# A two-layer gating and Mamba-2 trunk: scan chunks in pairs, split products in the order of their parts, and the output projection's scalings a part later

## The chip, the cores and the metric

The kernel runs on one core of one Trainium2 chip. The metric is the device time of one execution in microseconds (us). The engines have short names here: PE is TensorE's matmul, PEld its weight load, DVE is VectorE, ACT is ScalarE, POOL is GpSimd and SP is SyncE, which here only issues DMAs.

## The reference, cut to what matters

Two layers, each `h = h + W_out(mixer(rmsnorm(h)) * silu(z))`, and a final RMSNorm, on 1024 tokens of width 1024, all in float32. Layer A mixes by causal spatial gating in chunks of 128 tokens. Layer B is a Mamba-2 SSD mixer with 8 groups of 4 heads, a state of 128 and chunks of 128 tokens. What the change touches most is its scan, per group and chunk:

```python
cb = einsum('bclgn,bcsgn->bclsg', Cm, Bm)
w_ls = cb[..., None] * decay * dt[:, :, None]
y_diag = einsum('bclsgj,bcsgjp->bclgjp', w_ls, x)
states = einsum('bclgn,bclgj,bclgjp->bcgjpn', Bm, decay_to_end * dt, x)
# over the chunks: carry = carry * chunk_decay + state
y_off = einsum('bclgn,bcgjpn,bclgj->bclgjp', Cm, prev, exp(dA_cs))
y = y_diag + y_off + x * d_skip
gated = rmsnorm_per_group(y * silu(z))
out = gated @ w_out
```

## The kernel before, in words

Every float32 matrix product is made of three cheaper ones: both operands are split into a high part `h` and a low part `l` (`split`: ACT copies the high part, DVE or POOL subtracts it), and `mm3` issues hh, then h with one low part, then the other low part with h, for each piece of the contraction (L134, L135 and L136 of the profile). The large projections are not plain products either. `Block` (the input projections) and `Out` (the output projections `ao` of layer A and `bo` of layer B) use a scheme of seven half-size products (numbered 1 to 7) whose operands are sums of the blocks of the matrices; a product is worked in four parts `c` of 256 contraction rows, and the parts are prepared on ACT and DVE while PE is on an earlier one. `prep` splits a part's operands (L742 for DVE's half), `post` empties a product's accumulators.

The order is written by hand. Each engine executes its own list of instructions in the order in which the program issues them; nothing is moved by a scheduler. Buffers come from tagged pools: `sm` has four PSUM buffers, `k2` has four buffers for the decay tile `wl`, `q4` six, `k1` three for the state and `t1`.

The stages in time: a head (to 62 us), the blocks of layer A (to 530), its output projection `ao` (to 691), the passage to layer B and the first of its blocks (to 1007), the scan (to 1342), and the output projection `bo` with the final norm (to 1511). `scans` runs 64 chunks, eight groups of eight, and in between `project` issues what is left of layer B's input projection, in ticks of six products (`ab`), and then product 1 of `bo`. `want` says how many ticks are due after each half chunk. So PE's list alternates between a chunk's small float32 products and a few ticks.

For chunk `n`, before the change, the loop issues in this order: `pe_b(n)` (on PE the off-diagonal product with the state of the chunk before, L1626, the chunk's own state, L1633, and the diagonal, L1636, whose two heads of a pair go to the two column halves of the array; and in every fourth chunk the sums of squares, L1702), half a chunk of ticks, `pe_a(n+2)` (transposes and C.B, L1593 and L1594), `weights(n+1)` (DVE: `wl` times C.B, L1617), `update(n)` (DVE: the state, L1656), `out(n)` (DVE: L1668 and the skip L1671), `decay(n+2)` (ACT: L1599 and L1601), `carry(n+1)` (POOL, L1647), one `drain` of the convolution's queue (a tap on DVE is L1322), `tokens(n+2)` (DVE: L1607 and L1609) and `gate(n)` (POOL, L1674). Then SP gets `load(n+3)` (L1588: the decay of 128 columns spread over the partitions, 256 KB) and, in chunks 1 and 5 of a group, `prefetch` (`xbc`, 1 MB, L1554, for four of the groups; z, L1557; four spreads of exp(dA), L1561) for the next half group.

`hook_b` holds what `bo` does per product and part: loads (`get`), the scalings of its operands by the group norms (`ready`, L1755 on DVE), and sums of operand blocks (`plus`, `add`, L762).

Of the kernel before, what the change touches and what calls it, by code (L numbers as in the profile page):

```python
# [29 lines left out]
def kernel(  # L30
# [151 lines left out]
    class Block:  # L182
# [83 lines left out]
        def mm(self, n, i, post=True, halves=(0, 1)):  # L266
# [395 lines left out]
    class Out:  # L662
# [11 lines left out]
        def __init__(self, src, w, scale, res, accs, keep, order):  # L674
# [3 lines left out]
            self.Y3, self.negs = [], []  # L678
# [113 lines left out]
        def product(self, n, hook=None):  # L792
# [18 lines left out]
            for c in range(4):  # L811
# [45 lines left out]
        def last_mm(self, i):  # L857

            o = self.acc[3] = self.acc[5]
            Yh, Yl = zip(*self.Y3)  # L860
            if (3, i) not in self.ops:
                self.prep_unit(i)
            X = self.ops.pop((3, i))
            for k in range(8):
                mm3(o[i], [m[:, k, :] for m in X], [m[k // 4][:, k % 4, :] for m in (Yh, Yl)],
                    False, k == 7, True)
# [530 lines left out]
    def projections():  # L1397
# [21 lines left out]
        def push(g, kind, m, a):  # L1419
# [9 lines left out]
            if queue:  # L1429
                queue[-1] += ops.pop(0)  # L1430
# [118 lines left out]
    def prefetch(g, th):  # L1549

        st = sts[g]
        if g in xbc_d:
            t = st["xbc", th] = s8([P, 4, 512], "xbc")
            nc.sync.dma_start(out=t, in_=xbc_d[g][:, th])  # L1554
# [9 lines left out]
    class Scan:  # L1564


        def __init__(self, g, eng):
            self.g, self.st, self.eng = g, sts[g], eng
            self.wl, self.tp, self.cw, self.ps, self.state = {}, {}, {}, {}, {}
# [50 lines left out]
        def pe_b(self, c, ends=None):  # L1620

            w, wl = self.cw[c], self.wl.pop(c)
            yy = sm("yy")
            if c > 0:
                for pt in range(2):
                    nc.tensor.matmul(out=yy[:, 256 + pt * P:384 + pt * P],  # L1626
                                     lhsT=self.state[c - 1][:, pt * P:(pt + 1) * P], rhs=self.x(3, c),
                                     start=True, stop=True)
            sp = None
            if c < 7 or ends is not None:  # L1630
                sp = sm("sp")
            if c < 7:
                nc.tensor.matmul(out=sp[:, 0:256], lhsT=w[:, 512:640], rhs=w[:, 256:512], start=True, stop=True)  # L1633
            for j in range(4):
                pt, f = j // 2, j % 2
                nc.tensor.matmul(out=yy[f * 64:(f + 1) * 64, pt * P:(pt + 1) * P], lhsT=w[:, j * 64:(j + 1) * 64],  # L1636
                                 rhs=wl[:, j, :], start=True, stop=True)
            if ends is not None:
                ends.sum_b(sp[:, 256:512], 2 if ends.g == G - 1 else 1)
            self.ps[c] = yy, sp  # L1640
# [10 lines left out]
        def update(self, c):  # L1651
            if c == 0:
                self.state[0] = k1([P, 256], "state")
                V.tensor_copy(out=self.state[0], in_=self.ps[0][1][:, 0:256])
            elif c < 7:
                V.tensor_tensor(out=self.state[c], in0=self.ps[c][1][:, 0:256], in1=self.state[c], op=ALU.add)  # L1656
# [7 lines left out]
        def out(self, c):  # L1664
            yy, t2 = self.ps.pop(c)[0], self.y(c)
            if c > 0:
                t1 = k1([P, 2, P], "t1")
# [353 lines left out]
```

## Time and profile before

| What | us |
|---|---|
| median of 3 runs (range) | 1514.28 (1512.39 to 1514.48) |
| the profiled execution | 1512.85 |
| its span, first to last instruction | 1511.1 |
| PE busy in the span | 1471.6 (97%) |
| DVE, ACT, POOL busy | 1053.7, 783.3, 401.5 |
| PE's first matmul | 9.7 |

An engine's busy share says how much of the span it spent in instructions. PE's matmuls overlap, so a matmul row's duration (0.39 for 512 columns) is longer than the distance from one start to the next; distances between starts are what PE takes. A row of several records (`x8`) shows the start of the first. A bracket at a row's end gives the idle time ahead of it and the instruction whose end released it.

### The profile page before, as it was taken

The page shows a single profiled execution, that of the slowest core. Times are in us where ns is not written, and L with a number is a line of the kernel's source. Part 1 is how long each engine was busy: PE and PEld are TensorE (multiplying, and loading weights), DVE is VectorE, ACT ScalarE, POOL GpSimd, SP SyncE. Part 2 cuts the span into 40 slices and gives each one's busy share as a digit, 9 for nine tenths or more (in the row PEclk, how much of TensorE's full clock was granted, in tenths as well). Part 3 has the DMA queues.
Part 4 walks back from the last instruction along what each step waited for, and adds up shares of the span by engine and source line. Part 5 has one row for each costly group of instructions (what it writes and reads, how often), then busy time and mean ns, then how long its engine had stood idle before and what let it go on. Part 6 is the DMA issues. An engine that isn't in the chain of part 4 may idle for free. (4 is left out here: it accounts for less than half of the span.)

```text
span 1511.1 us, 21297 instructions
## 1 busy us (share of the span) xinstructions
PE 1471.6 (97%) x7834; PEld 1222.5 (81%) x7834; DVE 1053.7 (70%) x1713; ACT 783.3 (52%) x1256; POOL 401.5 (27%) x451
## 2 busy tenths in 40 slices
PE   6899999999999999999999999999999999999997
PEld 6899988888888888877878888877777777777875
DVE  7966567665666655678666467867677787688876
ACT  6533332222323445565565566666676666756463
POOL 1111110000000023202131222217576766633121
PEclk9999999999999999999999999999999999999999
DMA  5554322322222999957377978677655565579973
GB/s 183 141 168 140 106 97 103 117 103 103 101 79 96 337 262 246 258 145 162 104 174 154 208 154 167 142 242 209 183 160 183 160 187 141 169 255 275 255 156 112
DMA packets 174952, 254.45 MB, mean 168 GB/s; under 512 B 16400, under 2 KB 103168, under 8 KB 171648
## 3 DMA queue, kind: packets, MB, share of 16 engines
q1 hardware_dynamic: 124768, 168.93, 36.0%
q0 software_dynamic: 42448, 70.27, 23.2%
q10 hardware_dynamic: 7632, 13.90, 2.6%
q8 instruction: 62, 1.02, 0.3%
q14 instruction: 42, 0.34, 0.1%
HBM read 186.14 MB, written 51.18 MB: 157 GB/s over the span
## 5 line engine op out<-in xcount | busy, mean ns | idle before, releaser
L134 PE MATMUL acc<-hh,wh 128*128 128x512 f32 x868 | 339.9, 392 | 0.9 <-ACT u L296 0.9
L136 PE MATMUL acc<-hh,wl 128*128 128x512 f32 x868 | 338.4, 390 | 2.0 <-DVE wl L112 1.8
L135 PE MATMUL acc<-hl,wh 128*128 128x512 f32 x868 | 337.9, 389 | 0.0
L112 DVE TENSOR_TENSOR wl<-wr,wh 128x1024 fp32r<-128x1024 f32 (+1 forms) x96 | 114.3, 1193 | 118.3 <-ACT wh L111 118.1
L136 PEld LDWEIGHTS acc<-hh,wl 128*128 128x128 f32 x868 | 162.9, 188 | 37.9 <-DVE wl L112 3.7
L134 PEld LDWEIGHTS acc<-hh,wh 128*128 128x128 f32 x868 | 163.1, 188 | 34.9 <-ACT u L296 1.7
L135 PEld LDWEIGHTS acc<-hl,wh 128*128 128x128 f32 x868 | 163.1, 188 | 33.1
L296 ACT COPY u<-acc 128x512 f32<-128x512 f32 x115 | 66.8, 583 | 197.8 <-PE acc L136 197.7
L111 ACT CAST wh<-wr 128x1024 fp32r<-128x1024 f32 (+1 forms) x112 | 115.2, 1030 | 94.4 <-PE acc L135 56.9
L136 PE MATMUL acc<-wh,hl 128*128 128x256 f32 x448 | 129.2, 288 | 4.1 <-DVE hl L407 3.7
L134 PE MATMUL acc<-wh,hh 128*128 128x256 f32 x448 | 129.6, 289 | 2.9 <-DVE wh L418 1.3
L135 PE MATMUL acc<-wl,hh 128*128 128x256 f32 x448 | 128.5, 287 | 1.3 <-DVE wl L421 1.3
L134 PE MATMUL ab<-hh,wh 128*128 128x512 f32 x288 | 124.7, 433 | 1.2 <-DVE zt L999 0.7
L136 PE MATMUL ab<-hh,wl 128*128 128x512 f32 x288 | 113.2, 393 | 0.0
L135 PE MATMUL ab<-hl,wh 128*128 128x512 f32 x288 | 112.7, 391 | 0.0
L136 PEld LDWEIGHTS acc<-wh,hl 128*128 128x128 f32 x448 | 87.6, 196 | 5.4 <-DVE hl L407 4.4
L134 PEld LDWEIGHTS acc<-wh,hh 128*128 128x128 f32 x448 | 87.8, 196 | 3.8 <-ACT hh L400 1.6
L135 PEld LDWEIGHTS acc<-wl,hh 128*128 128x128 f32 x448 | 87.8, 196 | 1.7 <-DVE wl L421 1.5
L1599 ACT ACTIVATE wl<-wl,tk 128x128 f32<-128x128 f32 x256 | 81.6, 392 | 3.0 <-DMA wl<-cs_d 2.7
L649 POOL DMA_DIRECT2D y_d<-y x8 | 4.4, 549 | 290.8 <-DVE y L646 290.8
L135 PE MATMUL bo<-wl,xh 128*128 128x512 f32 x192 | 75.8, 395 | 3.8 <-DVE wl L742 2.1
L112 DVE TENSOR_TENSOR wl<-t,wh 128x1024 fp32r<-128x1024 f32 (+1 forms) x38 | 45.5, 1196 | 47.5 <-ACT wh L111 47.4
(317 smaller groups left out, 3250.6 us busy)
## 6 DMA issues: line engine op xcount, KB each, us to landing
wr<-in_a_w_in_dram SPq DMA_DIRECT2D x48, 512.0 KB, 3.6
wl<-cs_d SPq DMA_DIRECT2D x64, 256.0 KB, 3.6
wr<-in_b_w_in_dram SPq DMA_DIRECT2D x30, 512.0 KB, 7.4
wb<-in_a_w_out_dram SPq DMA_DIRECT2D x10, 1024.0 KB, 11.7
wb<-in_b_w_out_dram SPq DMA_DIRECT2D x10, 1024.0 KB, 11.1
wr<-in_b_w_in_dram SPq DMA_DIRECT2D x36, 256.0 KB, 5.9
v<-v_d SPq DMA_DIRECT2D x8, 1024.0 KB, 5.1
y_d<-y POOLq DMA_DIRECT2D x8, 1024.0 KB, 5.8
```

Source lines behind the costliest of these rows:

```text
L111: nc.scalar.copy(out=hi, in_=src)
L112: return (eng or nc.vector).tensor_tensor(out=lo, in0=src, in1=hi.bitcast(F32), op=ALU.subtract)
L134: nc.tensor.matmul(out=o, lhsT=l[0], rhs=r[0], start=start, stop=False, **kw)
L135: nc.tensor.matmul(out=o, lhsT=l[0], rhs=r[1], start=False, stop=False, **kw)
L136: nc.tensor.matmul(out=o, lhsT=l[1], rhs=r[0], start=False, stop=stop, **kw)
L296: nc.scalar.copy(out=self.u[n][:, i], in_=a)
L649: store = lambda: nc.gpsimd.dma_start(out=y_d[-1], in_=y)
L1599: nc.scalar.activation(wl[:, j, :], wl[:, j, :], AF.Relu, scale=-1.0, bias=tokc(2, c, self.g)[:, j:j + 1])
```

## The change

Four things are edited.

In `scans`, the chunks are issued in pairs. `pe_b` is taken apart into `own` (the state's product, L1658 after), `off` (L1667) and `diagonal`, which makes the eight products of two chunks in one row (L1650), with both chunks' results in one PSUM buffer. An even chunk issues own, off, the diagonal of itself and the next, the sums of squares where due, and the two loads of `wl` for chunks n+4 and n+5; an odd one own and off. `pe_a`, `decay` and `tokens` are now three chunks ahead, `weights` two, `update` stands ahead of `weights`, and `out` is split into `skip` and `out`. The even iteration drains the convolution's queue twice, as the odd one does. `prefetch` is split into two parts, the `xbc` part in the first chunk of each half group and the z and exp(dA) part in the second, both for the half group that starts four chunks after the first; `push` puts a convolution's first step ahead of, instead of behind, what the queue's last entry holds.

On SP the names are: `wl` the decay load, `wr` the raw weights of a later block, `xbc`, `ze` the z load and the spreads, `g_d` the gated output's store. Before, at the first chunks of the scan:

```order
L120 DMA wr<-in_b_w_in_dram 128x4x256
L1588 DMA wl<-cs_d 128x512 x3
L1554 DMA xbc<-xbc_d_6209 128x2048
L1557 DMA ze<-z_d_5287 128x2x512
L1561 DMA ze<-ecs_d 64x512 x4
L1588 DMA wl<-cs_d 128x512 x2
```

and now, at the same place:

```order
L120 DMA wr<-in_b_w_in_dram 128x4x256
L1610 DMA wl<-cs_d 128x512 x2
L1575 DMA xbc<-xbc_d_6209 128x2048
L1579 DMA ze<-z_d_5287 128x2x512
L1583 DMA ze<-ecs_d 64x512 x4
L1610 DMA wl<-cs_d 128x512 x4
```

Of the three `wl` loads that stood ahead of this `xbc` before, one, for chunk 4, takes a buffer that PE has to free, and it is chunk 0's; now both of the two do, and their buffers are those of the chunks 0 and 1, which the first paired diagonal reads.

On PE, two chunks of a spilled group before, from one chunk's products to the ticks behind them:

```order
L136 MATMUL ab<-hh,wl 128x512
L1626 MATMUL yy<-xbc,state 128x128 x2
L1633 MATMUL sp<-cw 128x256
L1636 MATMUL yy<-wl,cw 64x128 x4
L134 MATMUL ab<-hh,wh 128x512
```

and now, an odd chunk, the ticks and transposes behind it, and the even chunk that follows:

```order
L1658 MATMUL os<-cw 128x256
L1667 MATMUL os<-xbc,state 128x128 x2
L134 MATMUL ab<-hh,wh 128x512
L135 MATMUL ab<-hl,wh 128x512
L136 MATMUL ab<-hh,wl 128x512
L134 MATMUL ab<-hh,wh 128x512
L135 MATMUL ab<-hl,wh 128x512
L136 MATMUL ab<-hh,wl 128x512
L1615 MATMUL tp<-ident,xbc 128x128 x3
L1616 MATMUL tp<-xbc 128x128
```

```order
L136 MATMUL ab<-hh,wl 128x512
L1658 MATMUL os<-cw 128x256
L1667 MATMUL os<-xbc,state 128x128 x2
L1650 MATMUL yy<-wl,cw 64x128 x8
L134 MATMUL ab<-hh,wh 128x512
```

The diagonals' four products per chunk have become eight per pair, at the even chunk alone.

In `Block.mm`, `Out.product` and `Out.last_mm`, the three kinds of split product are no longer issued together for each contraction piece: all hh products of a part come first, then those with the part that is ready next, then the rest. In the last part of a product of `Out` the accumulators are finished one after the other.

In `hook_b`, for product 2, `ready(1, 0, c)` is put into a list `after` that `product` works off behind the preparation of the part, and the sum of the blocks of part `c` is made a part later. On DVE, around product 2's first parts (`ya` the gated operand that is scaled or summed, `xl` and `wl` the low parts of a part's operands), before:

```order
L1755 SCALAR_TENSOR_TENSOR ya<-ya,par,rb 128x512 x6
L762 TENSOR_TENSOR ya<-ya 128x1024
L742 TENSOR_TENSOR xl<-ya,xh 128x1024
L742 TENSOR_TENSOR wl<-wb,wh 128x1024
L1755 SCALAR_TENSOR_TENSOR ya<-ya,par,rb 128x512 x4
L762 TENSOR_TENSOR ya<-ya 128x1024
```

and now:

```order
L1786 SCALAR_TENSOR_TENSOR ya<-ya,par,rb 128x512 x2
L746 TENSOR_TENSOR xl<-ya,xh 128x1024
L746 TENSOR_TENSOR wl<-wb,wh 128x1024
L1786 SCALAR_TENSOR_TENSOR ya<-ya,par,rb 128x512 x4
L766 TENSOR_TENSOR ya<-ya 128x1024
L746 TENSOR_TENSOR xl<-ya,xh 128x1024
L746 TENSOR_TENSOR wl<-wb,wh 128x1024
```

Between two parts' low weights stood up to six scalings and a sum; now there are four and a sum.

The diff, cut to its core:

```diff
             if self.token_major:
-                for j in halves:
-                    s = slice((2 * i + j) * P, (2 * i + j + 1) * P)
-                    for k in range(4):
-                        mm3(o[:, j * 256:(j + 1) * 256], [Xh[:, k, s], Xl[:, k, s]], [y_[:, k, :] for y_ in Y],
-                            k == 0 and j == 0 and not more, k == 3, more or j == 1)
+                at = [(j, k) for j in halves for k in range(4)]
+                for X, y_, last in ((Xh, Y[0], False), (Xh, Y[1], False), (Xl, Y[0], True)):
+                    for j, k in at:
+                        s = slice((2 * i + j) * P, (2 * i + j + 1) * P)
+                        nc.tensor.matmul(out=o[:, j * 256:(j + 1) * 256], lhsT=X[:, k, s], rhs=y_[:, k, :],
+                                         start=X is Xh and y_ is Y[0] and k == 0 and j == 0 and not more,
+                                         stop=last and k == 3, skip_group_check=True)
             else:
                 m = slice(i * P, (i + 1) * P)
-                for k in range(4):
-                    mm3(o, [y_[:, k, m] for y_ in Y], [Xh[:, k, :], Xl[:, k, :]],
-                        k == 0 and not more, k == 3, more)
+                for X, y_, last in ((Xh, Y[0], False), (Xl, Y[0], False), (Xh, Y[1], True)):
+                    for k in range(4):
+                        nc.tensor.matmul(out=o, lhsT=y_[:, k, m], rhs=X[:, k, :],
+                                         start=X is Xh and y_ is Y[0] and k == 0 and not more,
+                                         stop=last and k == 3, skip_group_check=more)
...
                 low()
+                while self.after:
+                    self.after.pop(0)()
                 X, Y = self.ops.pop((n, c))
+                def mms(o=o, X=X, Y=Y, c=c):
+                    every = [(i, k) for i in range(4) for k in range(2)]
+                    if c < 3:
+                        seq3 = [(x_, y_, i, k) for x_, y_ in ((0, 0), (1, 0), (0, 1)) for i, k in every]
+                    else:
+                        seq3 = [(0, 0, i, k) for i, k in every] + \
+                            [(x_, 1 - x_, i, k) for i in range(4) for x_ in (1, 0) for k in range(2)]
+                    for x_, y_, i, k in seq3:
+                        nc.tensor.matmul(out=o[i], lhsT=X[x_][:, k, i * P:(i + 1) * P], rhs=Y[y_][:, k, :],
+                                         start=not more and c == 0 and k == 0 and x_ == y_,
+                                         stop=c == 3 and k == 1 and y_ == 1, skip_group_check=True)
+                        yield
+
+                todo = mms()
                 for i in range(4):
-                    for k in range(2):
-                        mm3(o[i], [m[:, k, i * P:(i + 1) * P] for m in X], [m[:, k, :] for m in Y],
-                            not more and c == 0 and k == 0, c == 3 and k == 1, more)
+                    for _ in range((12, 4, 4, 4)[i] if c == 3 else 6):
+                        next(todo)
...
-                queue[-1] += ops.pop(0)
+                queue[-1][:0] = ops.pop(0)
...
-    def prefetch(g, th):
+    def prefetch(g, th, part):
 
         st = sts[g]
-        if g in xbc_d:
-            t = st["xbc", th] = s8([P, 4, 512], "xbc")
-            nc.sync.dma_start(out=t, in_=xbc_d[g][:, th])
+        if part == 0:
+            if g in xbc_d:
+                t = st["xbc", th] = s8([P, 4, 512], "xbc")
+                nc.sync.dma_start(out=t, in_=xbc_d[g][:, th])
+            return
...
-        def pe_b(self, c, ends=None):
-
-            w, wl = self.cw[c], self.wl.pop(c)
+        def diagonal(self, c):
+
             yy = sm("yy")
+            for e in range(2):
+                w, wl = self.cw[c + e], self.wl.pop(c + e)
+                self.yy[c + e] = yy[:, e * 256:(e + 1) * 256]
+                for j in range(4):
+                    pt, f = j // 2, j % 2
+                    nc.tensor.matmul(out=self.yy[c + e][f * 64:(f + 1) * 64, pt * P:(pt + 1) * P],
+                                     lhsT=w[:, j * 64:(j + 1) * 64], rhs=wl[:, j, :], start=True, stop=True)
+
...
-            bo.ready(1, 0, 0)
...
-            if c < 3:
-                bo.ready(1, 0, c + 1)
-            (bo.plus if c < 2 else bo.add)(bo.a(0, 0, c), bo.a(1, 0, c))
+            bo.after.append(lambda: bo.ready(1, 0, c))
+            if c:
+                (bo.plus if c < 3 else bo.add)(bo.a(0, 0, c - 1), bo.a(1, 0, c - 1))
...
-        prefetch(0, 0)
+        prefetch(0, 0, 0), prefetch(0, 0, 1)
         project(AHEAD // 2 + 1)
         while todo or late:
             convolve()
-        for n in range(2):
+        for n in range(4):
             at("load", n)
         drain(1)
         for n in range(2):
             at("decay", n)
         drain(len(queue))
         at("pe_a", 0), at("tokens", 0), at("weights", 0)
+        at("pe_a", 1), at("tokens", 1), at("weights", 1)
         drain(len(queue))
         project(AHEAD)
-        at("pe_a", 1), at("tokens", 1), at("weights", 1)
-        at("load", 2)
+        at("decay", 2)
+        at("pe_a", 2), at("tokens", 2)
...
-            at("pe_b", n, scan[p] if c % 4 == 3 and p >= 0 else None)
-            project(want(n + .5))
-            at("pe_a", n + 2)
-            if n > 0:
-                at("weights", n + 1)
-            at("update", n)
-            at("out", n)
-            at("decay", n + 2)
-            at("carry", n + 1)
-            drain()
-            at("tokens", n + 2)
-            at("gate", n)
+            if c % 2 == 0:
+                at("own", n), at("off", n)
+                at("diagonal", n)
+                if c % 4 == 0 and g > 0:
+                    scan[g - 1].sum_b()
+                elif n == N - 2:
+                    scan[g].sum_b(n=2)
+                at("load", n + 4), at("load", n + 5)
+                project(want(n + .5))
+                at("pe_a", n + 3)
+                at("update", n)
+                at("carry", n + 1)
+                at("weights", n + 2)
+                at("decay", n + 3)
+                at("skip", n)
+                at("out", n)
+                at("skip", n + 1)
+                drain()
+                at("tokens", n + 3)
+                at("gate", n)
+                if c % 4 == 0 and g > 0:
+                    scan[g - 1].sum_c(1 if c else 0)
+                drain()
+            else:
+                at("own", n), at("off", n)
+                project(want(n + .5))
+                at("pe_a", n + 3)
+                at("update", n)
+                at("carry", n + 1)
+                at("weights", n + 2)
+                at("out", n)
+                drain()
+                at("decay", n + 3)
+                at("tokens", n + 3)
+                at("gate", n)
+                drain()
...
-            at("load", n + 3)
...
-            if c == 1:
-                prefetch(g, 1)
-            if c == 5 and g < G - 1:
-                prefetch(g + 1, 0)
+            k = n + 4
+            if c % 4 < 2 and k < N:
+                prefetch(k // 8, k // 4 % 2, c % 4)
```

More of the change, by code (lines that the diff above doesn't have):

```diff
@@ L863, in last_mm @@
             X = self.ops.pop((3, i))
-            for k in range(8):
-                mm3(o[i], [m[:, k, :] for m in X], [m[k // 4][:, k % 4, :] for m in (Yh, Yl)],
-                    False, k == 7, True)
+            for x_, y_, last in ((X[0], Yh, False), (X[0], Yl, False), (X[1], Yh, True)):
+                for k in range(8):
+                    nc.tensor.matmul(out=o[i], lhsT=x_[:, k, :], rhs=y_[k // 4][:, k % 4, :], start=False,
+                                     stop=last and k == 7, skip_group_check=True)
         def post(self, n, i):
@@ L1805, in hook_b @@
                 get("a", 1, 1, 3)
+                bo.add(bo.a(0, 0, 3), bo.a(1, 0, 3))
             if c < 2:
```

58 lines of the change are left out of this document (27 added, 31 removed).

## The prediction

> **What bounds the kernel now.** I read the page's busy line first, then the busy time by stage, then the timeline of TensorE (PE) inside the stages that the change touches, with the waits of its weight loads (PEld), and last SyncE's (SP) DMA issues beside their first use. The busy line and three stages (the head, the scan, products 2 and 7 of the second output projection; start and length, then busy us and instructions by engine, clock, DMA share, GB/s):
>
> ```profile
> PE 1471.6 (97%) x7834; PEld 1222.5 (81%) x7834; DVE 1053.7 (70%) x1713; ACT 783.3 (52%) x1256; POOL 401.5 (27%) x451
> ...
> 0.00:62.00 62.00, 43.49 (x301) 41.18 (x302) 49.53 (x91) 40.18 (x72) 10.00 (x16) 0.92 0.60 172
> 1007.00:1342.00 335.00, 332.65 (x2033) 258.56 (x2031) 246.48 (x509) 233.32 (x483) 220.24 (x247) 1.00 0.62 180
> 1366.00:1412.00 46.00, 43.93 (x192) 35.72 (x192) 39.15 (x49) 24.78 (x25) 10.96 (x12) 1.00 1.04 251
> ```
>
> PE sets the end nearly everywhere: 332.65 of 335 us in the scan, while VectorE (DVE) has 246.48, or 74%. A gain must come from PE's own time there, or from the places where it stands still: 18.5 us in the head, 2.1 in the third row. And PE's busy time is not all work; here is part of a scan chunk on PE.
>
> ```profile
> 1101.12 0.39 PE L1594 MATMUL tp<-bc 128*128 128x128 f32 x2
> 1101.26 0.48 PE L134 MATMUL ab<-hh,wh 128*128 128x512 f32 x1
> 1101.58 0.39 PE L135 MATMUL ab<-hl,wh 128*128 128x512 f32 x1
> ...
> 1102.74 0.59 PE L1633 MATMUL sp<-cw 128*128 128x256 f32 x2
> 1103.26 0.66 PE L1636 MATMUL yy<-wl,cw 128*64 128x128 f32 x8
> 1103.85 0.50 PE L134 MATMUL ab<-hh,wh 128*128 128x512 f32 x1
> 1104.18 0.39 PE L135 MATMUL ab<-hl,wh 128*128 128x512 f32 x1
> 1104.41 0.39 PE L136 MATMUL ab<-hh,wl 128*128 128x512 f32 x1
> ```
>
> Columns are start, duration, engine, line, operation, tiles, the array's shape, the operand's and the count. A 512-column product starts every 0.23 us (1104.18 to 1104.41). L1636 is the only one of these lines that uses half the array's columns (128*64), and round it the starts are wider apart.
>
> **The change, part by part.**
>
> *Pairing the diagonals.* A 128-column record of the scan takes 0.11 to 0.12: from 1101.12 to 1101.58 two such records and one product take 0.46, which is 2 x 0.115 + 0.23; so going from the one kind of product to the other costs nothing. Round L1636 it is otherwise. Its eight records fill half the columns two at a time, 8 x 0.055 = 0.44 (an estimate from 0.11), and take 0.59: 0.15 over. The product behind them takes 0.33 to the next: 0.10 over. L1633's two records of 256 columns ahead of them should take 4 x 0.11 = 0.44 and take 0.52: 0.08 over. A switch costs 0.33 us. The count, and what PEld waits for round it (us in all, times, longest):
>
> ```profile
> L1636 PE MATMUL yy<-wl,cw x512: 272/273/324, 1018.4 to 1350.4; 128*64 128x128 f32 x171
> ```
>
> ```profile
> PEld yy L1636 <- issue: 15.6, 47, 0.3
> PEld ab L134 <- issue: 12.5, 58, 0.4
> ```
>
> 512 records of eight are 64 switches; in pairs there are 32. The two waits on "issue" put 0.33 (15.6 / 47) and 0.22 (12.5 / 58) on the weight loads of one switch, some of it beside PE's work, so 0.55 is the upper end and 0.25 (without the way in) the lower. Removed: 32 x 0.33 = **-10.6 us** (-8 to -17.6). The records themselves stay.
>
> *Half a pair ahead.* Scan stalls of PE, as groups (the end of a row is the idle time and what ended it), and one of the places:
>
> ```profile
> L134 PE MATMUL ab<-hh,wh 128*128 128x512 f32 x273 | 118.8, 435 | 0.5 <-DVE x L1322 0.4
> L1626 PE MATMUL yy<-xbc,state 128*128 128x128 f32 x112 | 17.1, 275 | 0.9 <-DVE state L1656 0.8
> L1626 PE MATMUL yy<-bc,state 128*128 128x128 f32 x108 | 16.5, 275 | 0.4 <-DVE state L1656 0.3
> ```
>
> ```profile
> 1086.49 0.40 PE L136 MATMUL ab<-hh,wl 128*128 128x512 f32 x1
> 1087.69 0.68 PE L1626 MATMUL yy<-xbc,state 128*128 128x128 f32 x4 [0.80 <-DVE state L1656]
> ...
> 1088.74 0.44 PE L1636 MATMUL yy<-wl,cw 128*64 128x128 f32 x4
> ```
>
> The three idle times sum to 1.8 us; by starts it is more (1086.49 to 1087.69 is 1.20 for a pitch of 0.23, 0.97 lost beside 0.80 shown), and groups with less are left out here, so 2 to 4. The state's sum is now issued on DVE ahead of the weights' multiplication, the tokens a chunk earlier, and the sum of squares comes later: these go, **-3**. What can be late next is DVE: the queue is drained twice an iteration, so up to three convolution taps stand close together, one of them ahead of a state:
>
> ```profile
> L1322 DVE SCALAR_TENSOR_TENSOR x<-ab,par,x 128x1023 f32<-128x1023 f32 (+2 forms) x24 | 30.6, 1276 | 9.4 <-ACT x L1328 9.3
> ```
>
> One tap is 1.28 us, and DVE's idle quarter of a chunk of 5.2 us (335 / 64) covers one; I put **+1** (0 to +6) on it.
>
> *The loads on SP.* This is the step that speaks against the change. Before, the queue runs ahead of PE; its issues and the first use of what they bring:
>
> ```profile
> 1019.11 0.32 SPq L1588 DMA_DIRECT2D wl<-cs_d  x1
> 1019.48 0.43 SPq L1554 DMA_DIRECT2D xbc<-xbc_d  x1
> ```
>
> ```profile
> 1030.47 0.49 PE L1593 MATMUL tp<-ident,xbc 128*128 128x128 f32 x3
> ```
>
> ```profile
> L1554 SPq DMA_DIRECT2D xbc<-xbc_d x7: 427/599/1045, 1019.5 to 1236.5; - x7
> ...
> DMA to landing us min/median/max: 11.8/11.8/11.8
> ```
>
> ```profile
> v<-v_d SPq DMA_DIRECT2D x8, 1024.0 KB, 5.1
> ```
>
> The lead is 11 us, two chunks (1019.48 to 1030.47). There are four buffers for wl. The loads of chunks n+4 and n+5 now stand right behind the diagonals of n and n+1 and need the buffers that these read, so SP waits for PE there, and xbc is queued behind both. From the diagonals' end to the first transposes on the new xbc PE has 18 products of 0.23 (4.1), the way out of the switch (0.3), one chunk's five transposing records (5 x 0.11) and the next chunk's own and off products (1.05, 1087.69 to 1088.74): 6.0 us, or 7.4 where six more products fall in between; I take 6.5. The two wl issues take 0.37 each (1019.11 to 1019.48), so xbc goes out 0.7 after the end. Its landing is bounded by the 5.1 of another load of 1 MB and by 11.8, the one landing of an xbc that the profile measures. I take 7.5, nearer to 5.1, since the rest of the prefetch is now issued a chunk later and no longer shares the engines with it. It lands at 8.2 and PE stands for 8.2 - 6.5 = 1.7 us, seven times: **+11.9** (0 at 5.1, +42 at 11.8).
>
> Do such stalls cost the clock as well? The head's rows, below, say that several gaps close together do: after a last one of 1.46 us the 256-column starts go from 0.12 apart (43.46 to 43.58) to 0.21 (43.99 to 44.20). The third stage above holds a lone gap of 1.75 and keeps a granted clock of 1.00. So a lone 1.7 is priced without it. The Trainium skill (TensorE: Matmul & The Clock Gate, Part 1: The HAM clock gate) puts the array at half rate after an idle window of about 3.4 us; by that rule this sum stays as it is, while stalls beyond 3.4 us, as in rival (b), would each add an estimated 1.7 us, half of such a window at half rate, 12 in all.
>
> *Split products by readiness.* The products need the low part of a split last or in the middle instead of third. Two of the places:
>
> ```profile
> 43.24 0.38 PE L136 MATMUL acc<-wh,hl 128*128 128x256 f32 x1 [1.46 <-DVE hl L407]
> 43.46 0.28 PE L134 MATMUL acc<-wh,hh 128*128 128x256 f32 x1
> 43.58 0.28 PE L135 MATMUL acc<-wl,hh 128*128 128x256 f32 x1
> ...
> 43.99 0.42 PE L135 MATMUL acc<-wl,hh 128*128 128x256 f32 x1
> 44.20 0.42 PE L136 MATMUL acc<-wh,hl 128*128 128x256 f32 x1
> ```
>
> ```profile
> 991.56 0.50 PE L136 MATMUL acc<-hh,wl 128*128 128x512 f32 x1 [1.32 <-DVE wl L112]
> ...
> 994.85 0.47 PE L134 MATMUL ab<-hh,wh 128*128 128x512 f32 x1 [0.73 <-DVE zt L999]
> ```
>
> At the head (43.49 busy of 62) the same DVE chain feeds the next part, so most of the 1.46 returns there: -0.8 (0 to -2). The 1.32 at 991.56 goes, but DVE's zt is then waited for at 994.85: with small ones, -1.5 (-0.7 to -2.3). At a product's end the four accumulators are now finished 4 x 0.23 apart instead of 6 x 0.23, so a copy or a sum may hold up the next product by some tenths: 0 (to +2).
>
> *Output projection.* Product 2 stands still for the low part of the weights, behind six scalings on DVE (the second fence):
>
> ```profile
> 1371.06 0.39 PE L134 MATMUL bo<-wh,xh 128*128 128x512 f32 x1
> 1373.20 0.50 PE L135 MATMUL bo<-wl,xh 128*128 128x512 f32 x1 [1.75 <-DVE wl L742]
> ```
>
> ```profile
> 1365.67 4.06 DVE L1755 SCALAR_TENSOR_TENSOR ya<-ya,par,rb 128x512 f32<-128x512 f32 x6
> ```
>
> ```profile
> PEld bo L135 <- DVE wl L742: 2.9, 2, 2.2
> PEld bo L135 <- DVE wl L112: 2.2, 4, 0.8
> ```
>
> The low weights are now needed after eight products, 7 x 0.23 = 1.6 us later, and two of the scalings with their sum come a part later: the 2.14 - 0.23 = 1.9 at 1373.20 and the smaller one go, -2.5, and product 1's four shorter waits -1.3: **-3.8** (-1.5 to -4.5). The later products keep their time.
>
> Sum: -10.6 - 3 + 1 + 11.9 - 0.8 - 1.5 - 3.8 = -6.8 on the profiled execution's 1512.85 (its span of 1511.1 and 1.75 round it): 1506.1. The median of the runs, 1514.28, is 1.4 above that execution, so 1507.5; the rivals are given by the median too.
>
> **The rivals.**
>
> (a) *The loads come in time.* If xbc lands in 5 to 6 us, the +11.9 falls away: -18.7, 1495.6. For it: v's 5.1 for the same 1 MB. Against it: the only xbc whose landing is measured took 11.8.
>
> (b) *Slower: xbc's queue becomes the path.* At a landing of 10 us PE stands for 10.7 - 6.5 = 4.2 us seven times, +29.4 in place of 11.9: +10.7, 1525.0. It decides from a landing of 8.9 us on (7 x 3.1 us eats the 18.7 and 3 more). For it: the 11.8. Against it: that xbc had the prefetch's other loads right behind it, and these now come a chunk later.
>
> (c) *DVE gives the switches back.* If the bunched taps hold a state back by 0.8 us once in each of the eight groups, about +7 in place of +1 (0.8 x 8, and the 1): -0.8, 1513.5. For it: the state was what PE waited for at 1087.69. Against it: DVE has 88 of 335 us to spare.
>
> **How the numbers follow.** A measurement of this kernel tells 0.2%, 3 us, from no change. The forecast gets 0.45, with 1502 to 1513 for itself (landings of 6.7 to 8.3): 0.35 of it is faster, 0.08 the same, 0.02 slower. (a) gets 0.20, all faster. (b) 0.17, all slower. (c) 0.18: 0.03 faster, 0.10 same, 0.05 slower. Sums: 0.58, 0.18, 0.24. The range, 1493 to 1524, holds (a) with two more us of switches, the forecast, (c) and the near half of (b).
>
> **What would show it.** The diagonals' records should come in 32 groups of sixteen, with one switch of 0.33 us for each. The transposes on xbc should wait for DMA seven times, 1 to 3 us each, with xbc issued under 1 us behind the diagonals: no such wait is (a), four us or a half clock (b). In product 2 the 1.75 should be gone. A state or a convolution tap named as releaser of PE more than twice is (c). I am wrong if PE's starts round the diagonals are no nearer per chunk, or if the time leaves 1493 to 1524.

## The result, and the profile after

| kernel | median us (range, runs) | ratio to before (95%) |
|---|---|---|
| before | 1514.28 (1512.39 to 1515.99, 5) | |
| changed | 1520.86 (1520.26 to 1527.29, 5) | 1.0055 (1.0039 to 1.0072) |

The changed kernel is 6.6 us slower, where 6.8 us faster was forecast. Its profiled execution took 1520.26 us, of which 1518.6 are the span. The page's busy line, and the scan's stage in the stretch that the prediction showed of before (start and length, then busy us and instructions of PE, PEld, DVE, ACT and POOL, granted clock, DMA share, GB/s):

```profile
PE 1462.3 (96%) x7834; PEld 1230.6 (81%) x7834; DVE 1048.3 (69%) x1713; ACT 783.0 (52%) x1256; POOL 402.0 (26%) x451
```

```profile
1007.00:1342.00 335.00, 316.89 (x1979) 259.91 (x1979) 236.25 (x497) 229.68 (x474) 217.61 (x245) 0.99 0.60 172
```

PE was busy 332.65 of these 335 us before and is 316.89 now: it stands still for 18 us instead of 2.4, and the granted clock is 0.99 instead of 1.00. The largest of its waits, in the list of waits of the scan (us in all, times, longest):

```profile
PE tp L1615 <- DMA xbc<-xbc_d: 15.6, 7, 3.1
```

So the step that the prediction called the one against the change is where the time went: seven waits of the transposes for xbc. Here is the first of them on SP and on PE, and then the time from issue to landing of those xbc loads for which the profile measures one:

```profile
1018.56 0.80 SPq L1610 DMA_DIRECT2D wl<-cs_d  x2
1019.40 0.69 SPq L1575 DMA_DIRECT2D xbc<-xbc_d  x1
```

```profile
1017.86 1.09 PE L1650 MATMUL yy<-wl,cw 128*64 128x128 f32 x16
1018.89 0.50 PE L134 MATMUL ab<-hh,wh 128*128 128x512 f32 x1
...
1024.36 0.40 PE L136 MATMUL ab<-hh,wl 128*128 128x512 f32 x1
1027.85 0.55 PE L1615 MATMUL tp<-ident,xbc 128*128 128x128 f32 x3 [3.08 <-DMA xbc<-xbc_d]
```

```profile
DMA to landing us min/median/max: 5.8/6.4/6.9
```

The two wl loads go out while the diagonals run, xbc 0.5 us behind their end (1018.89 to 1019.40), and PE is ready for it at 1024.6, 5.2 us after the issue, where before it came 11 us after. And the last of the seven, in the later groups:

```profile
1237.88 0.80 SPq L1610 DMA_DIRECT2D wl<-cs_d  x2
1241.00 0.50 SPq L1740 DMA_DIRECT2D ss_d<-gsq  x1
1241.56 0.39 SPq L1575 DMA_DIRECT2D xbc<-xbc_d  x1
```

```profile
1238.10 0.60 PE L1733 MATMUL pr<-gsq,ones 128*64 128x256 f32 x4
1238.63 0.50 PE L134 MATMUL ab<-hh,wh 128*128 128x512 f32 x1
...
1244.09 0.40 PE L136 MATMUL ab<-hh,wl 128*128 128x512 f32 x1
1247.52 0.52 PE L1615 MATMUL tp<-ident,xbc 128*128 128x128 f32 x3 [3.04 <-DMA xbc<-xbc_d]
...
1248.59 0.63 PE L135 MATMUL ab<-hl,wh 128*128 128x512 f32 x1
1249.01 0.63 PE L136 MATMUL ab<-hh,wl 128*128 128x512 f32 x1
```

Here xbc goes out 3.5 us behind the diagonals' end (1238.10, where the sums of squares start, to 1241.56). A third command stands ahead of it, the store of the sums of squares (`ss_d`), which waits for ACT's copy of what PE has just summed. It stands there at five of the seven places; at the second place two loads of `wr` stand there, at the first nothing more. And the wait leaves something behind: the products start 0.42 apart (1248.59 to 1249.01) instead of 0.23. This is what half clock means here; it lasts until about 1251.

The other places. The split order removes the low parts' waits in the blocks, and PE comes to the scan's first tick earlier, but there it waits for DVE's zt (the sum that empties the last accumulator of the blocks), and runs on at half clock:

```profile
992.30 0.76 PE L134 MATMUL ab<-hh,wh 128*128 128x512 f32 x1 [2.79 <-DVE zt L1019]
992.86 0.63 PE L135 MATMUL ab<-hl,wh 128*128 128x512 f32 x1
993.29 0.63 PE L136 MATMUL ab<-hh,wl 128*128 128x512 f32 x1
```

In the output projection product 2's stop of 1.75 is gone, but PE now stops at the starts of product 7's parts, at product 6's start and ahead of the last step:

```profile
1405.52 0.73 PE L837 MATMUL bo<-wh,xh 128*128 128x512 f32 x2 [0.41 <-ACT wh L111]
...
1412.16 0.73 PE L837 MATMUL bo<-wh,xh 128*128 128x512 f32 x2 [0.89 <-ACT wh L111]
...
1419.21 0.47 PE L837 MATMUL bo<-wh,xh 128*128 128x512 f32 x1 [1.23 <-DVE u L900]
...
1486.90 0.93 PE L885 MATMUL bo<-yh,wh 128*128 128x512 f32 x3 [1.35 <-DVE u L908]
```

ACT is late for a reason of its own. Its operand is a sum that an accumulating DMA on POOL's queue makes:

```profile
1403.48 1.05 ACT L111 CAST xh<-ya 128x1024 fp32r<-128x1024 f32 x1 [7.65 <-DMA ya<-ya]
...
1410.11 1.05 ACT L111 CAST xh<-ya 128x1024 fp32r<-128x1024 f32 x1 [4.64 <-DMA ya<-ya]
```

```profile
1392.33 0.84 POOL L763 DMA_DIRECT2D ya<-ya  x1 [2.13 <-DVE ya L1786]
...
1398.74 0.84 POOL L763 DMA_DIRECT2D ya<-ya  x1 [4.70 <-DVE ya L1786]
```

The two DMAs are issued 1.7 us ahead of product 7's start (1394.07) and 4.7 behind it.

### The profile page after: what moved, and what is told of

It is laid out like the page before. It is cut to its first block, busy times and chain, and to the rows that moved or that the text cites. A ratio compares the mean times of both kernels' runs of the same rounds, so it can differ in the third digit from the quotient of the medians.

```text
span 1518.6 us, 21343 instructions
## 1 busy us (share of the span) xinstructions
PE 1462.3 (96%) x7834; PEld 1230.6 (81%) x7834; DVE 1048.3 (69%) x1713; ACT 783.0 (52%) x1256; POOL 402.0 (26%) x451
## 3 DMA queue, kind: packets, MB, share of 16 engines
q8 instruction: 62, 1.02, 0.3%
## 5 line engine op out<-in xcount | busy, mean ns | idle before, releaser
L289 PE MATMUL acc<-hh,wh 128*128 128x512 f32 x868 | 235.4, 392 | 0.9 <-ACT u L300 0.9
L289 PE MATMUL acc<-hh,wl 128*128 128x512 f32 x868 | 232.2, 389 | 0.0
L289 PE MATMUL acc<-hl,wh 128*128 128x512 f32 x868 | 232.2, 389 | 0.0
L112 DVE TENSOR_TENSOR xl<-ya,xh 128x1024 fp32r<-128x1024 f32 x36 | 44.1, 1225 | 40.5 <-ACT xh L111 35.3
L134 PEld LDWEIGHTS ab<-hh,wh 128*128 128x128 f32 x288 | 55.4, 192 | 18.5 <-issue 7.9
L282 PE MATMUL acc<-wh,hh 128*128 128x256 f32 x448 | 64.9, 287 | 3.8 <-ACT hh L402 1.8
L282 PE MATMUL acc<-wh,hl 128*128 128x256 f32 x448 | 64.2, 286 | 4.0 <-DVE hl L411 4.0
L1639 DVE TENSOR_TENSOR wl<-wl,cw 128x512 f32<-128x512 f32 x64 | 61.9, 967 | 6.2 <-ACT wl L1623 5.7
L282 PE MATMUL acc<-wl,hh 128*128 128x256 f32 x448 | 65.2, 288 | 0.3 <-DVE wl L425 0.3
L136 PEld LDWEIGHTS ab<-hh,wl 128*128 128x128 f32 x288 | 55.0, 191 | 12.9
```

What stands on the lines that cost most here:

```text
L112: return (eng or nc.vector).tensor_tensor(out=lo, in0=src, in1=hi.bitcast(F32), op=ALU.subtract)
L134: nc.tensor.matmul(out=o, lhsT=l[0], rhs=r[0], start=start, stop=False, **kw)
L136: nc.tensor.matmul(out=o, lhsT=l[1], rhs=r[0], start=False, stop=stop, **kw)
L282: nc.tensor.matmul(out=o[:, j * 256:(j + 1) * 256], lhsT=X[:, k, s], rhs=y_[:, k, :], start=X is Xh and y_ is Y[0] and k == 0 and j == 0 a ...
L289: nc.tensor.matmul(out=o, lhsT=y_[:, k, m], rhs=X[:, k, :], start=X is Xh and y_ is Y[0] and k == 0 and not more, stop=last and k == 3, sk ...
L1639: V.tensor_tensor(out=wl, in0=wl, in1=self.cw[c][:, 640:768].unsqueeze(1).broadcast_to([P, 4, P]), op=ALU.mult)
```

## The experiments

The theory after the result: the pairs gain what was forecast, and xbc, queued behind commands that wait for PE, costs more than that. The rival: xbc is slow for the traffic, whatever its place.

**xbc first.** One kind of command is moved on SP: each load of xbc goes ahead of the two wl loads.

```diff
+                if c % 4 == 0 and n + 4 < N:
+                    prefetch((n + 4) // 8, (n + 4) // 4 % 2, 0)
                 at("load", n + 4), at("load", n + 5)
...
-            if c % 4 < 2 and k < N:
-                prefetch(k // 8, k // 4 % 2, c % 4)
+            if c % 4 == 1 and k < N:
+                prefetch(k // 8, k // 4 % 2, 1)
```

> The changed kernel, with one DMA issue moved: the load of xbc (1 MB) is issued ahead of the two loads of wl that wait for PE's diagonal, instead of behind them. Theory (xbc lost its lead because it queues on SP behind two loads that wait for PE): the eight waits of the transposes for xbc, 19.1 us by the waits of PE and PEld, are gone or under 0.3 us each, and so are the stretches at half clock behind two of them (1.3 and 1.6 us): 1520.9 - 19 = 1500 to 1504. Rival (xbc lands late because the DMA engines are busy, 5.8 to 6.9 us whatever its place): the waits stay at 1 us or more in most of the seven places, and the time stays over 1514.

Measured: 1501.37 us (1498.11 to 1502.23, five runs), ratio to before 0.9911 (0.9900 to 0.9923); 19.5 us under the changed kernel. The first xbc on SP and its use on PE:

```profile
1012.98 0.46 SPq L1575 DMA_DIRECT2D xbc<-xbc_d  x1
1017.55 0.80 SPq L1610 DMA_DIRECT2D wl<-cs_d  x2
```

```profile
1023.59 0.49 PE L1615 MATMUL tp<-ident,xbc 128*128 128x128 f32 x3
```

The lead is 10.6 us again, and 10.6 to 16.2 at the seven places. All that PE waits for in the scan up to 1320 us is this:

```profile
PE bo L837 <- DVE wl L1639: 1.1, 1, 1.1
PE tp L1615 <- ACT bc L1453: 1.0, 1, 1.0
PE bo L837 <- ACT wh L111: 0.3, 1, 0.3
```

The stage's clock is 1.00. The theory holds, the rival falls: the same bytes in the same loop come in time, if they don't queue behind a command that waits. How long xbc takes to land here is not measured, since nothing waits for it.

**Unpaired.** On xbc first, the diagonals are again issued at each chunk, with the load and the skip that belong to it.

```diff
             else:
                 at("own", n), at("off", n)
+                at("diagonal", n)
+                at("load", n + 4)
                 project(want(n + .5))
```

> xbc first, and the diagonals again at each chunk (64 switches of the array's shape in place of 32), with their wl load and skip in their own chunk; the rest is as changed. Theory (a switch costs 0.33 us of PE): 10.6 us over the kernel with xbc first (9 to 12). Rival (what the pairs save is lost beside other work): under 4 us over it.

Measured: 1513.37 us (1510.34 to 1518.26, twelve runs), 12.0 over xbc first. Its profile holds one stop of 1.4 us for ACT's cw (at 1169.92) that xbc first has not, so 10.6 to 12.0 us are 32 switches: 0.33 to 0.37 each, against 0.33 in the sum. The runs of one kernel lie 4 to 8 us apart, so these are middle values and not bounds. A chunk of it on PE:

```profile
1108.24 0.66 PE L1652 MATMUL yy<-wl,cw 128*64 128x128 f32 x8
1108.83 0.50 PE L134 MATMUL ab<-hh,wh 128*128 128x512 f32 x1
```

Eight records take 0.59 here, and sixteen in the pair 1.03 (1017.86 to 1018.89 above): 1.03 - 0.59 = 0.44 for the second eight. The 0.15 that the first eight take on top is paid once.

**Pairs only.** The kernel before with the scan in pairs and xbc first; split products and product 2's scalings and sums as before.

```diff
-            at("pe_b", n, scan[p] if c % 4 == 3 and p >= 0 else None)
...
+            if c % 2 == 0:
+                at("own", n), at("off", n)
+                at("diagonal", n)
...
+                if c % 4 == 0 and n + 4 < N:
+                    prefetch((n + 4) // 8, (n + 4) // 4 % 2, 0)
+                at("load", n + 4), at("load", n + 5)
```

> The kernel before with only the scan in pairs, and xbc first; the split products, product 2's scalings and sums as before. Theory (the pairs are worth 11.5 us of switches and 2.6 of stops, less 2.5 of new waits for the last taps and the z part): 11 to 13 us under the kernel before. Rival (the scan's gain needs the new order of the products beside it): under 8.

Measured: 1503.13 us (1501.53 to 1503.43, five runs), ratio 0.9922 (0.9910 to 0.9934): 11.2 under before. The pairs with a timely xbc are three quarters of the 15.0 us that the fastest version gains.

**Scalings and sums undone.** On xbc first, `hook_b` as before.

```diff
-            bo.after.append(lambda: bo.ready(1, 0, c))
-            if c:
-                (bo.plus if c < 3 else bo.add)(bo.a(0, 0, c - 1), bo.a(1, 0, c - 1))
+            if c < 3:
+                bo.ready(1, 0, c + 1)
+            (bo.plus if c < 2 else bo.add)(bo.a(0, 0, c), bo.a(1, 0, c))
```

> xbc first, and in product 2 of bo the scalings and the sum of the operand blocks as in the kernel before (made in the part itself). Theory (the sums of blocks that product 7 needs are moved a part later, and their accumulating DMAs land late): product 7's waits of ACT for ya's DMA (7.7 and 4.6 us) shrink, the stops of PE at the starts of its parts (0.6, 1.1) and at the next product's start (1.4) go, product 7 takes 22 us instead of 25.1; product 2 is up to 1.5 us longer; together 1.5 to 2.5 us under the kernel with xbc first. Rival (the stops come from the order of the split products): product 7 stays at 25 and the time is the same or 1 us longer.

Measured: 1499.32 us (1498.91 to 1499.5, four runs), 2.05 under xbc first. POOL's two accumulating DMAs:

```profile
1369.70 0.91 POOL L763 DMA_DIRECT2D ya<-ya  x1
1372.00 1.15 POOL L763 DMA_DIRECT2D ya<-ya  x1
```

They stand 6.2 and 3.9 us ahead of product 7's start at 1375.86; PE makes product 7 in 21.8 us (1375.86 to 1397.62), where xbc first takes 24.1 (1372.94 to 1396.99) and the changed kernel 25.1 (1394.07 to 1419.21). Product 2 takes 23.9, against 23.7 in both of these: its waits for the low parts are gone, and it waits for ACT's high parts instead. So the edit in `hook_b` costs 2 us; the runs of the two versions overlap, but the rows of product 7 say the same.

**Sums with the scalings.** On xbc first, the scalings stay where the change puts them, the sum follows right behind them.

```diff
-            if c:
-                (bo.plus if c < 3 else bo.add)(bo.a(0, 0, c - 1), bo.a(1, 0, c - 1))
+            bo.after.append(lambda: (bo.plus if c < 2 else bo.add)(bo.a(0, 0, c), bo.a(1, 0, c)))
```

> xbc first; product 2's scalings stay behind the part's preparation as changed, but the sum of the blocks follows right behind them in the same part instead of a part later. Theory (the two sums that are accumulating DMAs on POOL's queue are what product 7 waits for): they are issued some 5 us earlier, ACT's waits for ya's DMA in product 7 fall from 7.7 and 4.6 to under 4, PE's stops at its parts go: 1.5 to 2.5 us under the kernel with xbc first (1501.4). Rival (the scalings themselves come too late): PE's stops in product 7 stay over 1 us, the time within 1 us of it.

Measured: 1499.49 us (1497.37 to 1501.66, five runs), 1.9 under xbc first, with ranges that overlap. ACT's waits between 1365 and 1405 us:

```profile
ACT xh L111 <- DMA ya<-ya: 8.4, 2, 4.5
```

This settles less than it was meant to. PE's stops in product 7 are gone, but stops of 1.3 and 1.7 us for ACT's high parts stand in product 2 instead; from product 1's start to product 6's it is 79.6 us against 80.2 of xbc first and 78.0 with both undone. The DMAs were not issued 5 us earlier, but 0.9 (2.6 us ahead of product 7's start and 3.8 behind it, against 1.7 and 4.7): they wait for DVE's scalings, which the change had moved as well. So the cost belongs to the scalings and sums moved together; how it divides between them stays open.

**Parts undone.** On xbc first, `Out.product` issues its split products with `mm3` again.

```diff
+                for i in range(4):
+                    for k in range(2):
+                        mm3(o[i], [m[:, k, i * P:(i + 1) * P] for m in X], [m[:, k, :] for m in Y],
+                            not more and c == 0 and k == 0, c == 3 and k == 1, more)
```

> xbc first, and in the products of ao and bo the three kinds of split product as in the kernel before (three to each contraction piece); the last step of each and the input blocks keep the new order. Theory (the accumulators are all finished within the last part's end, so the copies and sums of a product's end stand ahead of the next product): the stop of 1.4 us at product 6's start shrinks under 0.5 and the 1.5 us ahead of the last step under 0.9, product 1's waits for low parts return with 1.3 us and product 2's with 1: within 1.5 us of the kernel with xbc first. Rival (the new order is a clear gain in bo, hidden only by the sums): 3 us or more slower.

Measured: 1502.00 us (1498.1 to 1504.51, six runs), 0.6 over xbc first: no difference that these runs can tell. As expected, the stop ahead of product 6 is gone and 0.2 is left of the one ahead of the last step, while waits for low parts are back, 2.2 us in product 1 and 1.7 in product 2.

**Last part by accumulator.** On scalings and sums undone, the last part of a product finishes one accumulator at a time.

```diff
-                        seq3 = [(0, 0, i, k) for i, k in every] + \
-                            [(x_, 1 - x_, i, k) for i in range(4) for x_ in (1, 0) for k in range(2)]
+                        seq3 = [(x_, y_, i, k) for i in range(4) for x_, y_ in ((0, 0), (1, 0), (0, 1)) for k in range(2)]
```

> xbc first, product 2's scalings and sums as before, and in the last part of each product of ao and bo each accumulator worked to its end on its own (six products each, its three kinds in the new order), so the first is finished after 6 instead of 12 products and the last ones stand 6 apart instead of 4. Theory (the stops at the ends of products come from accumulators that are all finished late): the 1.5 us ahead of the last step falls to 0.4 or less and the 0.6 at product 6's start goes: 1.2 to 2.2 us under the kernel without this edit (1499.3). Rival (DVE and ACT are late there whatever the order): the stops stay, the same time.

Measured: 1499.32 us (1499.11 to 1501.18, four runs), the same as without it, and the stop ahead of the last step stays:

```profile
1466.04 1.16 PE L884 MATMUL bo<-yh,wh 128*128 128x512 f32 x4 [1.37 <-DVE u L907]
```

My theory on the ends of products falls, the rival holds: DVE is late there, whatever the order in which PE finishes. With the old order (pairs only) the same time is lost a few parts earlier:

```profile
1452.63 0.50 PE L135 MATMUL bo<-wl,xh 128*128 128x512 f32 x1 [0.69 <-DVE stats L911]
...
1469.76 0.47 PE L134 MATMUL bo<-yh,wh 128*128 128x512 f32 x1 [0.23 <-DVE u L890]
```

From product 5's start to the last step it is 23.7 us with the old order (1446.11 to 1469.76) and 23.2 to 23.3 with the new ones (1442.52 to 1465.75, 1442.75 to 1466.04): the order moves the wait, it doesn't remove it.

**Blocks undone.** On xbc first, `Block.mm` with `mm3` again (the token-major case likewise).

```diff
-                for X, y_, last in ((Xh, Y[0], False), (Xl, Y[0], False), (Xh, Y[1], True)):
...
+                for k in range(4):
+                    mm3(o, [y_[:, k, m] for y_ in Y], [Xh[:, k, :], Xl[:, k, :]],
+                        k == 0 and not more, k == 3, more)
```

> xbc first, and in the input blocks the three kinds of split product as in the kernel before; the output projections keep the new order. Theory (what the order gains in the blocks is handed back at the next wait, that of the first scan tick for DVE's zt): the stops for low parts at 716, 870 and 991 us return with 0.3, 0.7 and 1.5, the wait for zt falls from 2.5 to about 0.9, the head changes by under 1: 0 to 2 us over the kernel with xbc first (1501.4). Rival (a gain of its own, 2.3 as forecast and more): 3 us or more over it.

Measured: 1501.96 us (1500.78 to 1503.0, four runs), 0.6 over xbc first. PE's way to the scan:

```profile
991.88 0.50 PE L136 MATMUL acc<-hh,wl 128*128 128x512 f32 x1 [1.32 <-DVE wl L112]
...
995.69 0.47 PE L134 MATMUL ab<-hh,wh 128*128 128x512 f32 x1 [1.24 <-DVE zt L1015]
996.00 0.39 PE L135 MATMUL ab<-hl,wh 128*128 128x512 f32 x1
996.23 0.40 PE L136 MATMUL ab<-hh,wl 128*128 128x512 f32 x1
```

The low part's 1.32 is back, zt's wait is 1.24 instead of the 2.33 of xbc first, and the clock stays whole behind it (0.23 from 996.00 to 996.23), as it does in the profile of xbc first. The theory holds.

**Blocks, scalings and sums undone.** The diffs of "scalings and sums undone" and of "blocks undone" together, on xbc first.

> xbc first, product 2's scalings and sums as before, and the input blocks' split products in the order of the kernel before. Theory (in the blocks PE only gains the way to the wait for zt, and a wait of 2.2 us or more there can be followed by half clock): the wait for zt is 1 to 1.5 us, no half clock behind it, and the time is within 1.5 us of the kernel with the new order (1499.3). Rival (the blocks' order is a gain of its own): 2.3 us or more over it.

Measured: 1500.45 us (1499.52 to 1501.35, four runs), 1.1 over the kernel with the new order in the blocks; by the ratios to the kernel before the two are level (0.9904 and 0.9902). zt's wait is 1.18, and no half clock follows, where with the new order it is 2.72 and the half clock lasts until 998.9. So the order of the blocks brings no gain here that these runs can tell.

**Split order alone.** The kernel before with the new order in blocks, products and last step.

```diff
-                    for k in range(2):
-                        mm3(o[i], [m[:, k, i * P:(i + 1) * P] for m in X], [m[:, k, :] for m in Y],
-                            not more and c == 0 and k == 0, c == 3 and k == 1, more)
+                    for _ in range((12, 4, 4, 4)[i] if c == 3 else 6):
+                        next(todo)
```

> The kernel before, with only the new order of the split products (blocks, products, last step). Theory (the order takes the waits for low parts away, and gives some of it back at the ends of products and at zt): 1 to 3 us under the kernel before. Rival (the sum as forecast, 0.8 + 1.5 + 1.3 and the 2 us of product 2): 5 us or more under it.

Measured: 1515.33 us (1512.14 to 1519.37, twelve runs), ratio 1.0005 (0.9996 to 1.0013). Neither the 1 to 3 us of the theory nor the 5 of the rival. The profiled execution is the slowest of the twelve, so its rows show where time can be lost and not what is lost each time. The first place is zt's:

```profile
992.83 0.77 PE L134 MATMUL ab<-hh,wh 128*128 128x512 f32 x1 [2.96 <-DVE zt L1017]
993.40 0.63 PE L135 MATMUL ab<-hl,wh 128*128 128x512 f32 x1
993.82 0.63 PE L136 MATMUL ab<-hh,wl 128*128 128x512 f32 x1
```

PE starts there 2.0 us earlier than before (994.85), and the half clock that follows lasts until 998.9, fourteen products, some 2.8 us lost. The larger place is the start of product 1, at the scan's end:

```profile
1336.83 1.22 PE L835 MATMUL bo<-wh,xh 128*128 128x512 f32 x2 [3.56 <-ACT z L1441]
1337.85 1.05 PE L1644 MATMUL yy<-bc,state 128*128 128x128 f32 x4
```

With all hh products first, the fifth of them needs the third accumulator, which ACT's z has still to empty; with the old order the third accumulator is needed after twelve products. PE stands for 3.56 us and goes on at half clock (two products in 1.02), 5 us lost together. The same stop is 1.1 us in the changed kernel, and no profile with the old order in the products has it:

```profile
1340.33 0.74 PE L837 MATMUL bo<-wh,xh 128*128 128x512 f32 x2 [1.13 <-DVE wl L1639]
```

```profile
1339.25 1.02 ACT L1443 ACTIVATE z<-ab 128x1024 f32<-128x1024 f32 x1
```

The bracket names DVE's wl, whose end (1340.32) is 0.05 behind that of ACT's z (1340.27); that z is what holds PE is read from the program and was not tested by a run.

The versions add up so: before 1514.3, the pairs with xbc in time 1503.1, with the split order 1499.3, with scalings and sums moved 1501.4, with xbc behind the loads 1520.9. Three versions are the fastest and can't be told apart: xbc first with scalings and sums as before (1499.32), the same with the last part by accumulator (1499.32), and sums with the scalings (1499.49). The 3.8 us between pairs only and the first of these is what the split order is worth there; taken back piece by piece it was worth 0.6, 0.6 and 1.1, and on the kernel before nothing. Single runs of a kernel lie up to 8 us apart, so its worth stays open within some 3 us.

## Why the prediction was wrong, point by point

*Pairing the diagonals, -10.6*: right. Unpaired against paired is 10.6 to 12.0.

*Stalls that go, -3, and new ones, +1*: right in kind. No wait for a state or a tap is left in the scan. What is late next is not the taps on DVE but the end of a convolution on ACT, 1.0 us. Pairs only against before is 11.2, where this term and the one above had 12.6 together.

*The loads on SP, +11.9*: this is the step that failed, by its size. Mechanism, count and place were right: the lead is lost, seven transposes wait for DMA, 0.7 to 3.1 us each. The sum made each stop of three terms. By the starts of SP's and PE's rows, as means over the seven places, they are: from issue to the transposes' start 7.3 us (5.8 to 8.8) where I took 7.5; from the diagonals' end until PE is ready 7.1 (5.7 to 7.6) where I took 6.5; and from the diagonals' end to the issue 2.2 (0.5 to 3.5) where I took 0.7. So the issue is the term that was mis-sized, since at five places the store of the sums of squares had come between, and that waits for PE and ACT in turn. I had the rule that each queue is followed command by command, and stopped at the two loads. The stops come to 16.8 us by these starts. To this came the clock, which I priced at nothing for a stop of 1.7 us and which fell to half behind two of the longer ones, some 3 us. Together 19.5 instead of 11.9.

That the landing came out near 7.5 is in part luck. I put it near the lower bound because the rest of the prefetch would go out a chunk later. At three places it did not: SP went nearly straight on, and z's load went out 0.8 to 1.7 us behind xbc. There xbc took 7.1 to 8.8 us, and 5.8 to 7.8 at the four places where z went out 7 to 9 us behind it. No run separates the traffic from the place.

Of the 13.4 us between the forecast and the result the loads are 7.6. Split order and output projection are 4.4 (6.1 forecast; 3.8 less 2.05 came), the pairs with their stalls 1.4. These figures are differences of medians, so they hold within a few us.

*Split order, -0.8 - 1.5*: the waits for low parts went, as said, and PE was ready for the scan's first tick 4.6 us earlier, twice what was forecast (994.12 to 989.51, the tick's start less the idle time). But DVE's zt sets that point, as the quoted rows had shown: its wait grew from 0.73 to 2.79, so the tick started 2.55 earlier, and the half clock behind it took 1.5 of that (992.30 to 995.42 holds seven products, 3.12 - 7 x 0.23). What the sum didn't have at all is the new stop at the start of product 1, 1.1 us here and 3.56 in the split order alone.

*Output projection, -3.8*: the stop of 1.75 went, as said, but in product 2 only 0.8 came of it (24.5 us before, 23.7 now), since ACT's high part and another low part are late next (0.45 and 0.41). And product 7 lost 3.4 (21.8 to 25.1): the sums that I moved along in the sum of terms as work of DVE issue DMAs on POOL's queue, whose landing product 7 waits for. I had weighed the moved step by its DVE instructions alone.

*The rivals*: (b) had the mechanism and the sign, at a landing of 10 us; it came by the issue instead. (a)'s 1495.6 was the kernel without the waits for xbc; that one took 1501.4, 2.0 of the rest being `hook_b`. (c) did not happen.

*The page on the clock gate*: the Trainium skill (TensorE: Matmul & The Clock Gate, Part 1: The HAM clock gate) has the half rate after an idle window of about 3.4 us; by it, and by the lone gap of 1.75, I left the clock out of the sum. Here it fell behind eight lone gaps of 2.18 to 3.04 us and one of 3.56, and didn't behind gaps of 2.33, 2.51, 3.08 and 3.09. The page also says that the window runs free of the kernel, which agrees with so mixed an outcome; that a stop below the window's length leaves the clock alone is not borne out.

## What to carry to other kernels

A load's lead is set by what stands ahead of it in its queue: moved behind a command that waits for the consumer engine, a prefetch shrinks from two chunks of lead to one, and every further command in between that waits adds its own wait. Put the loads that wait for nothing ahead of those that wait for a buffer. And a wait removed ahead of a point that another engine sets comes back there in part, here 2.1 of 4.6 us, and a wait grown past some 2 us may cost the clock as well. An order that issues the ready operands first also needs every accumulator sooner: see that they are empty by then.

## What the runs showed of the hardware

A change of TensorE's column shape and back costs 0.33 to 0.37 us by two kernels that differ in 32 of them, though no wait but "issue" shows it. And the half clock can follow a single gap of little over 2 us between busy stretches (2.18 with parts undone, 2.31 in the changed kernel), and last from 3 to 6 us: 1.5 us lost behind the 2.79 of the changed kernel, 2.8 behind the 2.96 of the split order alone. Behind 2.33 in the kernel with xbc first, 2.51 unpaired and 3.08 and 3.09 in the changed kernel the clock stayed whole, and behind gaps of 1.9 us and less it fell in none of these scans.
